# A two-layer hybrid decoder trunk on one core: most tile transposes move from TensorE to VectorE and the DMA queues

## The chip, the cores and the metric

The kernel runs on one core of a Trainium2 chip. The metric is the device time of one execution in microseconds (us). A core has five engines that each take their instructions in order: TensorE (PE; PEld is its weight load), VectorE (DVE), ScalarE (ACT), GpSimd (POOL) and SyncE (SP), which here only issues DMA transfers. The engines wait for each other through semaphores. An instruction that waits holds up everything behind it on its own engine, and a transfer that waits in SP's program holds up every later transfer of SP.

## The reference

Two layers, 256 tokens, model width 2048, everything in float32. Each layer normalises `x`, multiplies it by one wide input projection, and uses the columns for two branches: attention in 16 heads (with query and key normalisation, rotary positions and a mixture of three dilated causal windows), and a causal convolution module (gated unit, depthwise convolution of width 31, layer norm, SiLU, pointwise projection). Both branches are normalised, gated and mapped back into the residual.

```python
for layer in range(DEPTH):
    h = rms_norm(x, norm_g[layer])
    proj = jnp.einsum("bsd,de->bse", h, w_in[layer])
    q, k, v, g_att, glu_a, glu_b, g_conv = jnp.split(proj, SPLIT_POINTS, axis=-1)
    q = apply_rope(rms_norm(q...), cos, sin); k = apply_rope(rms_norm(k...), cos, sin)
    att_y = rms_norm(dilated_mixture(q, k, v), att_out_g[layer]) * jax.nn.silu(g_att)
    conv = conformer_conv(glu_a, glu_b, dw_kernel[layer], ..., w_pw[layer])
    conv_y = rms_norm(conv, conv_out_g[layer]) * jax.nn.silu(g_conv)
    x = x + jnp.einsum("bse,ed->bsd", jnp.concatenate([att_y, conv_y], axis=-1), w_out[layer])
```

## The kernel before, in words

The weights are streamed once. They are cut into 640 tiles of 256 rows by 512 columns (512 KB); eight tiles make a group, which is one block of 512 output columns, and a layer has 40 groups. `load(i)` issues the transfer of tile i on SP into one of four `raw` buffers. `split(i)` turns it into a high part on ACT (`whi`) and a low part on DVE (`wlo`), in one of four pairs of buffers, and then issues `load(i + 4)` into the buffer that it has emptied. TensorE takes 12 matmuls of 512 columns for a tile (high by high, low by high, high by low; two row blocks; two halves of the tokens). The split runs three tiles ahead.

The activations are the stationary operand. They stand transposed, as high and low parts, in `st_hi` and `st_lo` (two sets of four chunks of 512 channels). To make them, and to make `qT`, `kT` and `uT` (the transposed gated unit that the convolution reads), `transposes` sends eight 128 x 128 blocks of a [256, 512] tile through TensorE into two PSUM banks, from which ACT and DVE read. There are 44 such calls: 24 for the gated unit, q and k (4 blocks j in 2 layers each), 8 for g_att, 8 for pw and 4 for the next layer's x.

The order of the groups in a layer is: for j = 0 to 3 the five groups glu_b, glu_a, v, q, k; then g_conv 0, g_att 0 to 3, g_conv 1 to 3, o_att 0 to 3, pw 0 to 3, o_conv 0 to 3. The result of a group is read from PSUM by its `ev_...` function. A group may start only when the group two before it has been read.

Everything that isn't the weight stream is cut into slices that a planner (`Filler`) places. A slice names what it costs on each engine (`Need(A=1.0)`: 1.0 us of ACT), a condition, and the PSUM banks it needs. After every tile the planner's `run` adds each slice that fits its estimate of the engines' clocks, in order of priority. `until` forces slices when the matmuls need their result at once. So the order of each engine's program is fixed when the kernel is built. The convolution (`conv`) has the lowest priority and fills DVE: per block j 124 operations of 128 x 256. When the last block is done, the layer norm follows: a sum over channels on POOL (`ysum`), a matmul with ones, the mean subtracted on DVE, squares on ACT, their sum on POOL (`ssum`, one copy and seven additions), four small matmuls with ones, the reciprocal root on POOL (`rstd`, copied out as `rbc`), two matmuls with `ident` that spread it, then on DVE and ACT the scaling, the SiLU and the parts for `st_hi[1]` and `st_lo[1]`, which the pw groups read. The rotary tables of the next layer are built on POOL with POOL's own transfers (`rope_tables`), and are issued where the code reaches them, at the end of the group o_att 3.

Of the kernel before, what the change touches and what calls it, by code (L numbers as in the profile page):

```python
# [10 lines left out]
F32 = mybir.dt.float32  # L11
F32R = mybir.dt.float32r
BF16 = mybir.dt.bfloat16
AF = mybir.ActivationFunctionType
# [16 lines left out]

KS = 2
NSTEP = KT // KS
R_RAW, R_SPLIT = 4, 4
AHEAD = 3

WARM = 14
# [13 lines left out]
class Filler:  # L51
# [94 lines left out]
def trunk(ctx: ExitStack, tc: tile.TileContext, x, w_in, q_norm_g, k_norm_g, w_pw, w_out, x_t, gains, params,  # L146
# [8 lines left out]
    def t(shape, name, dt=F32):  # L155
        return sb.tile(shape, dt, name=name)
# [13 lines left out]
    qT, kT = (C[i].rearrange("p (h s) -> p h s", h=4) for i in (1, 2))  # L170
    Dt = [t([128, 2, CH], f"d{i}") for i in range(3)]
    t2 = t([128, CH], "t2")
    sm = [t([128, 384], f"sm{i}") for i in range(4)]
    junk = t([128, CH], "junk", BF16)
    ident = t([128, 128], "ident")
# [66 lines left out]
    def has(*what):  # L242
        return lambda: what in flags
# [6 lines left out]
    def transposes(src, banks):  # L250

        for b in range(2):
            for i in range(2):
                for tt in range(2):
                    e = (2 * b + i) * 128
                    T.transpose(banks[b][:, i * SEQ + tt * 128:i * SEQ + tt * 128 + 128],  # L256
                                src[:, tt, e:e + 128], ident)

    def to_stationary(src, s, c, gain):
# [12 lines left out]
        filled(s, c)  # L272

    def filled(s, c):
        vacant[s][c] = False
        ready[s][c] = True
# [11 lines left out]

    def x_chunk(l, c):

        yield from to_stationary(A[c], 0, c, lambda i: ng[:, l * KT + 4 * c + i:l * KT + 4 * c + i + 1])
        fill.add(x_square(l, c), 3, fill.now[4])

    def x_square(l, c):
# [16 lines left out]
    def ev_glu_a(l, j, ps):  # L311
        yield Need(0, has("ev", l, "glu_b", j), V=1.4)
        for tt in range(2):
            V.scalar_tensor_tensor(Dt[0][:, tt], ps[tt], rx[:, tt:tt + 1], Dt[0][:, tt],
                                   op0=ALU.mult, op1=ALU.mult)
        flag("ev", l, "glu_a", j)
        yield Need(2, has("conv", l, j - 2) if j >= 2 else None, P=0.9)
        banks = [fill.bank(), fill.bank()]
        transposes(Dt[0], banks)
        yield Need(A=1.0)  # L320
        for b in range(2):
            S.activation(uT[j % 2][:, 2 * b:2 * b + 2, PAD:], banks[b].rearrange("p (c s) -> p c s", c=2), AF.Copy)
        fill.free(*banks)
        flag("glu", l, j)
        fill.add(conv(l, j), 5 + j, fill.now[4])

# [92 lines left out]
    def ev_qk(l, j, ps, nm):  # L419
        before = ("rope", l, j, "q") if nm == "k" else ("rope", l, j - 1, "k") if j else None  # L420
        yield Need(0, before and has(*before), A=2.8, G=2.3)
        for tt in range(2):
            for h in range(4):
                S.activation(junk[:, :DH], ps[tt][:, h * DH:(h + 1) * DH], AF.Square, scale=rx[:, tt:tt + 1],  # L424
                             accum_out=qss[:, tt, h:h + 1])
        a, b = (1.0, DH * EPS) if nm == "q" else (1.0 / DH, EPS)
        G.tensor_scalar(qr, qss, a, b, op0=ALU.mult, op1=ALU.add)  # L427
        G.tensor_tensor(qr, qr, half.rearrange("p (t h) -> p t h", t=2), op=ALU.pow)  # L428
        G.tensor_mul(qr, qr, rx[:, :, None].to_broadcast([128, 2, 4]))  # L429
        n = Dt[1]  # L430
        for tt in range(2):
            yield Need(A=1.2)
            for h in range(4):
                S.activation(n[:, tt, h * DH:(h + 1) * DH], ps[tt][:, h * DH:(h + 1) * DH], AF.Copy,  # L434
                             scale=qr[:, tt, h:h + 1])
        flag("ev", l, nm, j)
        o = Dt[2]
        for tt in range(2):
            yield Need(V=1.9)
            nt, ot = (z[:, tt].rearrange("p (h d) -> p h d", h=4) for z in (n, o))  # L440
            t2v = t2.rearrange("p (h d) -> p h d", h=4)
            ca, cb = rope[nm + "a"], rope[nm + "b"]
# [6 lines left out]
        banks = [fill.bank(), fill.bank()]  # L449
        transposes(o, banks)  # L450
        flag("rope", l, j, nm)
        yield Need(A=1.0)
        dst = qT if nm == "q" else kT
        for b in range(2):
            S.activation(dst[:, 2 * b:2 * b + 2], banks[b].rearrange("p (h s) -> p h s", h=2), AF.Copy)  # L455
        fill.free(*banks)
        if nm == "k":
            for h in range(4):
                fill.add(head(l, j, h), 2, fill.now[4])

    def head(l, j, h):
        yield Need(1, has("attn", l, j - 1) if j else None, P=0.7)
        ps = fill.bank()
        T.matmul(ps[:, 0:128], qT[:, h, 0:128], kT[:, h, 0:128], start=True, stop=True)  # L464
        T.matmul(ps[:, 128:384], qT[:, h, 128:256], kT[:, h, 0:256], start=True, stop=True)  # L465
        flag("qk1", l, j, h)
        if all(("qk1", l, j, k) in flags for k in range(4)):
            flag("qk", l, j)
# [48 lines left out]
    def ev_g_att(l, j, ps):  # L517
# [5 lines left out]
        yield from to_stationary(A[j], 0, j, lambda i: prm[:, 4 * j + i, P_ATT + l:P_ATT + l + 1])  # L523
# [9 lines left out]
    def ev_pw(l, j, ps):  # L533
# [6 lines left out]
        if j == NCH - 1:  # L540
# [4 lines left out]
        yield from to_stationary(y, 1, j, lambda i: prm[:, 4 * j + i, P_CONV + l:P_CONV + l + 1])  # L545

    def ev_o_conv(l, j, ps):
        yield Need(0, has("rc", l), V=1.4)
# [19 lines left out]
    load(2)  # L568
    nc.sync.dma_start(Y[2], x_t[:, 2])
    load(3)  # L570
    later = [(Y[3], x_t[:, 3], None)]
    later += [(A[c], x[0, :, c * CH:(c + 1) * CH].rearrange("(t p) e -> p t e", p=128), c) for c in range(NCH)]
    later.append((prm, params, None))
    make_identity(nc, ident)
    V.memset(half, -0.5)
# [113 lines left out]
```

## Time and profile before

| | |
|---|---|
| median of 3 runs | 1861.46 us (1860.73 to 1862.61) |
| the profiled execution | 1862.08 us, span 1860.3 us, mean granted TensorE clock 0.998 |
| busy | PE 1847.6 us, DVE 1392.2, ACT 989.2, POOL 140.2 |
| moved by DMA | 352.06 MB, mean 189 GB/s, queue q1 at 60.7% of 16 engines |

The matmuls are pipelined, so a busy PE isn't a PE at its peak; a better view is the chain of work that ended last, which gives the distance from one instruction to the next.

### The profile page before, as it was taken

The page shows a single profiled execution, that of the slowest core. Times are in us where ns is not written, and L with a number is a line of the kernel's source. Part 1 is how long each engine was busy: PE and PEld are TensorE (multiplying, and loading weights), DVE is VectorE, ACT ScalarE, POOL GpSimd, SP SyncE. Part 2 cuts the span into 40 slices and gives each one's busy share as a digit, 9 for nine tenths or more (in the row PEclk, how much of TensorE's full clock was granted, in tenths as well). Part 3 has the DMA queues.
Part 4 walks back from the last instruction along what each step waited for, and adds up shares of the span by engine and source line. Part 5 has one row for each costly group of instructions (what it writes and reads, how often), then busy time and mean ns, then how long its engine had stood idle before and what let it go on. Part 6 is the DMA issues. An engine that isn't in the chain of part 4 may idle for free.

```text
span 1860.3 us, 23725 instructions
## 1 busy us (share of the span) xinstructions
PE 1847.6 (99%) x8490; PEld 1535.9 (83%) x8490; DVE 1392.2 (75%) x2157; ACT 989.2 (53%) x1559; POOL 140.2 (8%) x153
## 2 busy tenths in 40 slices
PE   8999999999999999999999999999999999999999
PEld 6788888888888888888888888888888888888887
DVE  5788889788889876556558888797887998755554
ACT  5565564654654465445444655646556445644542
POOL 2010100200010141000000101002000102100000
PEclk9999999999999999999999999999999999999999
DMA  8765656656566676565666656565565666665564
GB/s 277 218 184 169 183 170 182 182 172 189 170 183 191 193 224 208 195 186 191 210 200 188 191 159 186 162 195 182 161 188 162 196 195 188 213 205 193 180 204 147
DMA packets 181527, 352.06 MB, mean 189 GB/s; under 512 B 11248, under 2 KB 11248, under 8 KB 181408
## 3 DMA queue, kind: packets, MB, share of 16 engines
q1 hardware_dynamic: 179584, 347.19, 60.7%
q0 software_dynamic: 960, 1.77, 0.5%
q8 instruction: 66, 1.08, 0.2%
q10 hardware_dynamic: 864, 1.59, 0.2%
q14 instruction: 53, 0.43, 0.1%
HBM read 346.31 MB, written 4.19 MB: 188 GB/s over the span
## 4 chain that ended last, share of the span: by engine, by line
PE 97%; DMA 1%; DVE 1%; ACT 0%; issue 0%; SPq 0%; POOL 0%; ACTq 0%; DVEq 0%
PE acc L619 92%; PE ax L256 2%; DMA raw<-in_w_in 1%; PE ax L465 1%; DMA a<-in_x 1%; PE ax L482 1%; PE ax L491 0%; PE ax L490 0%; PE ax L489 0%; PE ax L464 0%; DVE wlo L230 0%; ACT whi L229 0%; DVE stlo L285 0%; SPq L222 0%; ACT junk L297 0%
## 5 line engine op out<-in xcount | busy, mean ns | idle before, releaser
L230 DVE TENSOR_TENSOR wlo<-raw,whi 128x1024 fp32r<-128x1024 f32 x640 | 792.6, 1247 | 411.7 <-ACT whi L229 405.6
L229 ACT ACTIVATE whi<-raw 128x1024 fp32r<-128x1024 f32 x640 | 675.4, 1063 | 658.2 <-PE acc L619 468.4
L619 PE MATMUL acc<-whi,sthi 128*128 128x512 f32 x2560 | 823.9, 393 | 6.6 <-ACT sthi L283 5.8
L619 PE MATMUL acc<-wlo,sthi 128*128 128x512 f32 x2560 | 815.9, 390 | 0.8 <-DVE wlo L230 0.8
L619 PE MATMUL acc<-whi,stlo 128*128 128x512 f32 x2560 | 815.5, 390 | 0.0
L619 PEld LDWEIGHTS acc<-wlo,sthi 128*128 128x128 f32 x2560 | 481.2, 188 | 102.3 <-DVE wlo L230 1.8
L619 PEld LDWEIGHTS acc<-whi,stlo 128*128 128x128 f32 x2560 | 481.1, 188 | 100.8
L619 PEld LDWEIGHTS acc<-whi,sthi 128*128 128x128 f32 x2560 | 476.5, 188 | 102.8 <-ACT sthi L283 6.7
L339 DVE SCALAR_TENSOR_TENSOR y<-ut,prm,y 128x256 f32<-128x256 f32 x960 | 408.4, 482 | 0.0
L427 POOL TENSOR_SCALAR qr<-qss 128x8 f32<-128x8 f32 x16 | 3.2, 198 | 696.6 <-ACT junk L424 696.6
L347 POOL TENSOR_TENSOR ysum<-ysum,y 128x256 f32<-128x256 f32 x30 | 36.5, 1218 | 240.8 <-DVE y L339 133.5
L424 ACT ACTIVATE junk<-acc,rx 128x128 bf16<-128x128 f32 x128 | 47.1, 368 | 8.4 <-PE acc L619 4.8
L434 ACT ACTIVATE d<-acc,qr 128x128 f32<-128x128 f32 x128 | 34.8, 384 | 15.8 <-POOL qr L429 15.8
L267 ACT ACTIVATE sthi<-ax,prm 128x256 fp32r<-128x256 f32 x64 | 25.1, 476 | 30.7 <-PE ax L256 30.7
L269 DVE SCALAR_TENSOR_TENSOR stlo<-ax,prm,sthi 128x256 fp32r<-128x256 f32 x64 | 26.5, 475 | 14.4 <-ACT sthi L267 14.4
L455 ACT ACTIVATE c<-ax 128x512 f32<-128x512 f32 x32 | 17.4, 597 | 33.7 <-PE ax L256 33.7
L478 ACT ACTIVATE sm<-sm,smm 128x128 f32<-128x128 f32 x64 | 28.2, 443 | 6.6 <-DVE smm L473 6.6
L375 POOL TENSOR_TENSOR ssum<-ssum,d 128x512 f32<-128x512 f32 x14 | 28.5, 2034 | 6.5 <-ACT d L368 5.6
L428 POOL TENSOR_TENSOR qr<-qr,half 128x8 f32<-128x8 f32 x16 | 26.3, 1642 | 1.3
L256 PEld LDWEIGHTS ax<-ident,d 128*128 128x128 f32 x192 | 22.4, 140 | 3.2
L256 PE MATMUL ax<-ident,d 128*128 128x128 f32 x192 | 24.9, 273 | 0.0
L424 ACT ACTIVATION_READ_ACCUMULATOR junk<-acc,rx 128x1 f32 x128 | 24.7, 193 | 0.0
(105 smaller groups left out, 659.2 us busy)
## 6 DMA issues: line engine op xcount, KB each, us to landing
raw<-in_w_in SPq DMA_DIRECT2D x448, 512.0 KB, 4.1
raw<-in_w_out SPq DMA_DIRECT2D x128, 512.0 KB, 4.7
raw<-in_w_pw SPq DMA_DIRECT2D x64, 512.0 KB, 4.7
a<-in_x SPq DMA_DIRECT2D x8, 512.0 KB, 6.1
xs<-a SPq DMA_DIRECT2D x4, 512.0 KB, 7.0
a<-xs SPq DMA_DIRECT2D x4, 512.0 KB, 6.1
y<-in_x_t SPq DMA_DIRECT2D x3, 512.0 KB, 12.5
out<-a SPq DMA_DIRECT2D x4, 256.0 KB, 5.4
```

The lines of the kernel that those rows point to most:

```text
L229: S.activation(hi, a, AF.Copy)
L230: V.tensor_sub(wlo[i % R_SPLIT], a, hi.bitcast(F32))
L256: T.transpose(banks[b][:, i * SEQ + tt * 128:i * SEQ + tt * 128 + 128], src[:, tt, e:e + 128], ident)
L269: V.scalar_tensor_tensor(st_lo[s][c][:, i], p[i], gain(i), st_hi[s][c][:, i].bitcast(F32), op0=ALU.mult, op1=ALU.subtract)
L339: V.scalar_tensor_tensor(y[:, c], u[:, c, k:k + SEQ], w[:, c, l * CW + k:l * CW + k + 1], y[:, c], op0=ALU.mult, op1=ALU.add)
L347: G.tensor_add(ysum, ysum, y[:, c])
L375: G.tensor_add(ssum, ssum, half_sq)
L424: S.activation(junk[:, :DH], ps[tt][:, h * DH:(h + 1) * DH], AF.Square, scale=rx[:, tt:tt + 1], accum_out=qss[:, tt, h:h + 1])
L428: G.tensor_tensor(qr, qr, half.rearrange("p (t h) -> p t h", t=2), op=ALU.pow)
L434: S.activation(n[:, tt, h * DH:(h + 1) * DH], ps[tt][:, h * DH:(h + 1) * DH], AF.Copy, scale=qr[:, tt, h:h + 1])
L478: S.activation(s[:, cs], s[:, cs], AF.Exp, bias=m[:, tt:tt + 1], scale=-1.0, accum_out=lsum[:, tt:tt + 1])
L619: T.matmul(ps[tt], xl if n == 2 else xh, lo[:, kk] if n == 1 else hi[:, kk], start=(k == 0 and n == 0), stop=(k == KT - 1 and n == 2))
```

## The change

Of the 44 calls of `transposes`, 41 are replaced by `turn`; the three that stay are the last x chunk and pw 3 of both layers. (The words of the change count 296 of 320 blocks; in the code it is 328 of 352.) `turn` transposes the 32 x 32 squares inside a [256, 512] tile on DVE (two instructions, into the one buffer `blocks`), stores the result to DRAM with one transfer of 512 KB in rows of 1 KB, and brings it back with four loads of 128 KB, each of which puts one 32-row block of the squares at its place on all partitions. All five transfers are issued on SP. `turned` is the view in which the result is then read: its tokens lie in runs of 32. ACT and DVE read SBUF where they read PSUM; `kT` needs no copy, since the head matmuls read the loaded tile itself. A flag lets only one turn be between its transposes and its loads in the planner's order. The planner has a new clock, Q, for the exchange. Six `raw` buffers take the place of four, six tiles are loaded at the start, and the last chunk of `x_t` is loaded before them rather than among the later loads. The buffer for POOL's transfer descriptors is set to 4096.

```diff
-R_RAW, R_SPLIT = 4, 4
+R_RAW, R_SPLIT = 6, 4
...
-        self.t = dict(P=0.0, V=0.0, A=0.0, G=0.0)
+        self.t = dict(P=0.0, V=0.0, A=0.0, G=0.0, Q=0.0)
...
+    def turn(src, dst):
+        yield Need(0, lambda: not turns[1], V=1.4)
+        turns[1] = True
+        for tt in range(2):
+            V.transpose(blocks.rearrange("p (b c t j) -> p t c b j", b=4, c=4, t=2)[:, tt],
+                        src[:, tt].rearrange("p (c b j) -> p c b j", c=4, b=4))
+        yield Need(Q=6.0)
+        way = crossing[turns[0] % 2]
+        turns[0] += 1
+        nc.sync.dma_start(way.rearrange("b p x -> p b x"), blocks.rearrange("p (b x) -> p b x", b=4))
+        yield Need(Q=7.0)
+        turns[1] = False
+        for a in range(4):
+            nc.sync.dma_start(dst[:, a * SEQ:(a + 1) * SEQ], way[:, 32 * a:32 * a + 32])
+
+    def turned(z):
+        return z.rearrange("p (a c t j) -> p c t a j", a=4, c=4, t=2)
+
+    def to_stationary_turned(src, dst, s, c, gain):
+        yield from turn(src, dst)
+        yield Need(0, lambda: vacant[s][c], A=1.8, V=2.2)
+        z = turned(dst)
...
+        for i in range(4):
+            S.activation(hi[:, i], z[:, i], AF.Copy, scale=gain(i))
+        for i in range(4):
+            for tt in range(2):
+                V.scalar_tensor_tensor(lo[:, i, tt], z[:, i, tt], gain(i), hi[:, i, tt].bitcast(F32),
...
-        yield Need(2, has("qk", l, j - 1) if j else None, P=0.9)
-        banks = [fill.bank(), fill.bank()]
-        transposes(o, banks)
+        before = has("qk", l, j - 1) if j else None
+        if nm == "q":
+            z = o.rearrange("p t e -> p (t e)")
+            yield from turn(o, z)
+            yield Need(0, before, A=1.8)
+            for h in range(4):
+                S.activation(qT[:, h].rearrange("p (t a j) -> p t a j", t=2, a=4), turned(z)[:, h], AF.Copy)
+        else:
+            yield Need(0, before)
+            yield from turn(o, kT)
...
-    later = [(Y[3], x_t[:, 3], None)]
+    load(4)
+    nc.sync.dma_start(Y[3], x_t[:, 3])
+    load(5)
...
+    nc = bacc.Bacc("TRN2", target_bir_lowering=False, num_devices=1, dynamic_dma_scratch_size=4096)
```

Three places show how the planner's order comes out. The tiles are numbered through from 0; pw 0 of the first layer begins with tile 256.

First place: POOL's program in the first layer, from the sum of the layer norm (`ysum`, `ssum`) to `rbc`. Before:

```order
L347 TENSOR_TENSOR ysum<-ysum,y_84 128x256 x4
L373 COPY ssum<-d_108 128x512
L375 TENSOR_TENSOR ssum<-ssum,d_108 128x512
L375 TENSOR_TENSOR ssum<-ssum,d_109 128x512 x2
L375 TENSOR_TENSOR ssum<-ssum,d_108 128x512 x2
L375 TENSOR_TENSOR ssum<-ssum,d_109 128x512 x2
L247 TENSOR_SCALAR rstd<-rsc 128x2
L248 TENSOR_TENSOR rstd<-rstd,half 128x2
L389 COPY rbc<-rstd 128x256
L583 DMA ropeqa<-in_rope_cos 128x2x128
L586 DMA gbc<-in_q_norm_g 128x64 x2
L588 TENSOR_TENSOR ropeqa<-ropeqa,gbc 128x256
```

Now (of the rotary tables only the first and the last of the four are shown):

```order
L389 TENSOR_TENSOR ysum<-ysum,y_84 128x256 x4
L415 COPY ssum<-d_110 128x512
L417 TENSOR_TENSOR ssum<-ssum,d_110 128x512
L417 TENSOR_TENSOR ssum<-ssum,d_111 128x512 x2
L636 DMA ropeqa<-in_rope_cos 128x2x128
L639 DMA gbc<-in_q_norm_g 128x64 x2
...
L641 TENSOR_TENSOR ropekb<-ropekb,gbc 128x256
L417 TENSOR_TENSOR ssum<-ssum,d_110 128x512 x2
L417 TENSOR_TENSOR ssum<-ssum,d_111 128x512 x2
L251 TENSOR_SCALAR rstd<-rsc 128x2
L252 TENSOR_TENSOR rstd<-rstd,half 128x2
L431 COPY rbc<-rstd 128x256
```

Before, the sum and the root were whole ahead of the tables; now all four tables stand between its fourth and its fifth operation. In the second layer there are no tables to build, and the eight operations stand together.

Second place: PE's program at the layer norm's small matmuls (`ones,ssum` and `ident,rbc`). Before, in the group o_att 0 of the first layer, ahead of tile 227 (the second pair, not shown, stood ahead of tile 231):

```order
L619 MATMUL acc_153<-whi_95,stlo_74 128x512
L619 MATMUL acc_154<-whi_95,stlo_74 128x512
L383 MATMUL ax_158<-ones,ssum 128x2 x4
L619 MATMUL acc_153<-whi_96,sthi_66 128x512
L619 MATMUL acc_154<-whi_96,sthi_66 128x512
```

Now:

```order
L672 MATMUL acc_159<-wlo_102,sthi_68 128x512
L672 MATMUL acc_159<-whi_98,stlo_76 128x512
L425 MATMUL ax_161<-ones,ssum 128x2 x4
L435 MATMUL ax_162<-ident,rbc 128x128 x2
L672 MATMUL acc_156<-whi_95,sthi_69 128x512
L672 MATMUL acc_157<-whi_95,sthi_69 128x512
L672 MATMUL acc_156<-wlo_99,sthi_69 128x512
```

Both pairs now stand directly ahead of tile 256, whose first matmul reads `sthi_69`, the layer norm's own result; in the second layer they stand the same way ahead of tile 576. The matmul that sums `ysum` stood ahead of tile 216 (536) and stands ahead of tile 250 (570). On DVE the last operation of the convolution stood behind 215 splits of a layer's 320 and stands behind 249.

Third place: SP's program round the turn of k for j = 0 (`crossing` is the DRAM buffer, `c_107` is `kT`; the last load shown ahead of the store is that of tile 59):

```order
L226 DMA raw_93<-in_w_in 128x2x512
L226 DMA raw_94<-in_w_in 128x2x512
L275 DMA crossing_164<-blocks 128x4x256
L279 DMA c_107<-crossing_164 128x1x256 x4
L226 DMA raw_89<-in_w_in 128x2x512
L226 DMA raw_90<-in_w_in 128x2x512
```

Before, only weight loads stood here. The head matmuls that read `kT` stood one tile behind k's transposes on PE (the tile between them was 46); now they stand ahead of tile 56, and wait for the four loads. The pattern repeats every 40 tiles, eight times in all.

## Rows read from the trace of the kernel before

**Rows 1.** The page: busy us (share of the span) xinstructions, and DVE's largest group.
```profile
PE 1847.6 (99%) x8490; PEld 1535.9 (83%) x8490; DVE 1392.2 (75%) x2157; ACT 989.2 (53%) x1559; POOL 140.2 (8%) x153
L230 DVE TENSOR_TENSOR wlo<-raw,whi 128x1024 fp32r<-128x1024 f32 x640 | 792.6, 1247 | 411.7 <-ACT whi L229 405.6
```
**Rows 2.** The chain that ended last, by line: share of the span.
```profile
PE acc L619 92%; PE ax L256 2%; DMA raw<-in_w_in 1%; PE ax L465 1%; DMA a<-in_x 1%; PE ax L482 1%; PE ax L491 0%; PE ax L490 0%; PE ax L489 0%; PE ax L464 0%; DVE wlo L230 0%; ACT whi L229 0%; DVE stlo L285 0%; SPq L222 0%; ACT junk L297 0%
```
**Rows 3.** The chain in order of time, 640 to 720 us: start us, us, what.
```profile
643.73 0.43 PE ax L355 x2
649.65 0.87 PE ax L256 x8
650.52 5.49 PE acc L619 x24
...
677.72 0.79 PE ax L383 x8
...
689.51 0.45 PE ax L393 x4
```
**Rows 4.** Groups by form: busy us, mean ns of one, idle before (TensorE's transposes).
```profile
L256 PE MATMUL ax<-ident,d 128*128 128x128 f32 x192 | 24.9, 273 | 0.0
L256 PE MATMUL ax<-ident,a 128*128 128x128 f32 x96 | 12.4, 272 | 0.0
L256 PE MATMUL ax<-ident,y 128*128 128x128 f32 x64 | 8.3, 272 | 0.0
```
**Rows 5.** POOL's timeline, 630 to 800 us: start us, us, line, what, idle before.
```profile
652.71 0.61 POOL L373 COPY ssum<-d 128x512 f32<-128x512 f32 x1 [16.12 <-ACT d L368]
653.40 10.23 POOL L375 TENSOR_TENSOR ssum<-ssum,d 128x512 f32<-128x512 f32 x5
...
680.24 0.19 POOL L247 TENSOR_SCALAR rstd<-rsc 128x2 f32<-128x2 f32 x1 [9.42 <-DVE rsc L386]
...
681.62 0.81 POOL L583 DMA_DIRECT2D ropeqa<-in_rope_cos  x1
...
708.92 1.28 POOL L588 TENSOR_TENSOR ropekb<-ropekb,gbc 128x256 f32<-128x256 f32 x1 [3.16 <-DMA gbc<-in_k_norm_g]
```
**Rows 6.** Groups by form on DVE and ACT, whole span.
```profile
L443 DVE TENSOR_TENSOR d<-d,ropeqa 128x512 f32<-128x512 f32 x16 | 10.9, 681 | 0.0
L445 DVE TENSOR_TENSOR t<-d,ropekb 128x256 f32<-128x256 f32 x32 | 12.0, 417 | 0.0
L365 DVE TENSOR_TENSOR y<-y,nmean 128x1024 f32<-128x1024 f32 x8 | 9.8, 1271 | 0.0
L406 ACT ACTIVATE y<-y,prm 128x256 f32<-128x256 f32 x32 | 16.6, 590 | 1.3 <-DVE y L403 1.3
L409 ACT ACTIVATE sthi<-y 128x1024 fp32r<-128x1024 f32 x8 | 8.4, 1053 | 0.1
```
**Rows 7.** The page's DMA issues: xcount, KB each, median us to landing.
```profile
raw<-in_w_in SPq DMA_DIRECT2D x448, 512.0 KB, 4.1
xs<-a SPq DMA_DIRECT2D x4, 512.0 KB, 7.0
ropeka<-in_rope_cos POOLq DMA_DIRECT2D x2, 128.0 KB, 3.5
```
**Rows 8.** ACT's timeline, 244 to 256 us (k is read from PSUM).
```profile
245.97 0.37 ACT L424 ACTIVATE junk<-acc,rx 128x128 bf16<-128x128 f32 x1 [0.30 <-PE acc L619]
...
253.30 2.18 ACT L434 ACTIVATE d<-acc,qr 128x128 f32<-128x128 f32 x8 [1.54 <-POOL qr L429]
```
**Rows 9.** PE's first wait in the timeline, and busy time by window with clock, DMA share, GB/s.
```profile
19.70 1.22 PE L619 MATMUL acc<-whi,sthi 128*128 128x512 f32 x2 [3.66 <-ACT sthi L283]
20.00:30.00 10.00, 10.00 (x39) 8.13 (x39) 9.33 (x16) 7.00 (x14) 4.76 (x7) 0.87 0.94 311
```
**Rows 10.** ACT's timeline, 0 to 60 us: the second chunk of x.
```profile
36.86 0.63 ACT L297 ACTIVATE junk<-a 128x512 bf16<-128x512 f32 x1 [3.08 <-DMA a<-in_x]
```

More of the change, by code (lines that the diff above doesn't have):

```diff
@@ L169, in trunk @@
     VT = [GC[0], GC[3]]
-    qT, kT = (C[i].rearrange("p (h s) -> p h s", h=4) for i in (1, 2))
+    qT, kT = C[1].rearrange("p (h s) -> p h s", h=4), C[2]
     Dt = [t([128, 2, CH], f"d{i}") for i in range(3)]
     t2 = t([128, CH], "t2")
+    blocks = t([128, 2 * CH], "blocks")
     sm = [t([128, 384], f"sm{i}") for i in range(4)]
@@ L197, in trunk @@
     fill = Filler([pp.tile([128, CH], F32, name=f"ax{i}") for i in range(4)], dict(V=4.5, A=3.5), 5)
+    crossing = [dr.tile([4, 128, SEQ], F32, name=f"crossing{i}") for i in range(2)]
+    turns = [0, False]
     xs = [dr.tile([SEQ, CH], F32, name=f"xs{c}") for c in range(NCH)]
@@ L257, in transposes @@
                                 src[:, tt, e:e + 128], ident)
+    def turn(src, dst):
[18 more added lines that the diff above has]
+        z = turned(dst)
+        hi, lo = (o[s][c].rearrange("p c (t a j) -> p c t a j", t=2, a=4) for o in (st_hi, st_lo))
+        for i in range(4):
[3 more added lines that the diff above has]
+                V.scalar_tensor_tensor(lo[:, i, tt], z[:, i, tt], gain(i), hi[:, i, tt].bitcast(F32),
+                                       op0=ALU.mult, op1=ALU.subtract)
+        filled(s, c)
     def to_stationary(src, s, c, gain):
@@ L289, in x_chunk @@
     def x_chunk(l, c):
-        yield from to_stationary(A[c], 0, c, lambda i: ng[:, l * KT + 4 * c + i:l * KT + 4 * c + i + 1])
+        gain = lambda i: ng[:, l * KT + 4 * c + i:l * KT + 4 * c + i + 1]
+        if c < NCH - 1:
+            yield from to_stationary_turned(A[c], Y[c], 0, c, gain)
+        else:
+            yield from to_stationary(A[c], 0, c, gain)
         fill.add(x_square(l, c), 3, fill.now[4])
@@ L316, in ev_glu_a @@
         flag("ev", l, "glu_a", j)
-        yield Need(2, has("conv", l, j - 2) if j >= 2 else None, P=0.9)
-        banks = [fill.bank(), fill.bank()]
[L319 to L323, printed above, removed]
+        z = Dt[0].rearrange("p t e -> p (t e)")
+        yield from turn(Dt[0], z)
+        yield Need(0, has("conv", l, j - 2) if j >= 2 else None, A=1.7)
+        for c in range(4):
+            S.activation(uT[j % 2][:, c, PAD:].rearrange("p (t a j) -> p t a j", t=2, a=4), turned(z)[:, c], AF.Copy)
         flag("glu", l, j)
@@ L447, in ev_qk @@
             V.tensor_add(ot, ot, t2v)
-        yield Need(2, has("qk", l, j - 1) if j else None, P=0.9)
-        banks = [fill.bank(), fill.bank()]
-        transposes(o, banks)
-        flag("rope", l, j, nm)
[L452 to L456, printed above, removed]
+        before = has("qk", l, j - 1) if j else None
[5 more added lines that the diff above has]
+                S.activation(qT[:, h].rearrange("p (t a j) -> p t a j", t=2, a=4), turned(z)[:, h], AF.Copy)
+        else:
+            yield Need(0, before)
+            yield from turn(o, kT)
+        flag("rope", l, j, nm)
+        yield Need()
         if nm == "k":
@@ L463, in head @@
         ps = fill.bank()
-        T.matmul(ps[:, 0:128], qT[:, h, 0:128], kT[:, h, 0:128], start=True, stop=True)
-        T.matmul(ps[:, 128:384], qT[:, h, 128:256], kT[:, h, 0:256], start=True, stop=True)
+        k = turned(kT)[:, h]
+        T.matmul(ps[:, 0:128], qT[:, h, 0:128], k[:, 0], start=True, stop=True)
+        T.matmul(ps[:, 128:384], qT[:, h, 128:256], k, start=True, stop=True)
         flag("qk1", l, j, h)
@@ L522, in ev_g_att @@
         flag("ev", l, "g_att", j)
-        yield from to_stationary(A[j], 0, j, lambda i: prm[:, 4 * j + i, P_ATT + l:P_ATT + l + 1])
+        yield from to_stationary_turned(A[j], A[j].rearrange("p t e -> p (t e)"), 0, j,
+                                        lambda i: prm[:, 4 * j + i, P_ATT + l:P_ATT + l + 1])
         src = x[0, :, j * CH:(j + 1) * CH] if l == 0 else xs[j]
@@ L544, in ev_pw @@
             flag("rc", l)
-        yield from to_stationary(y, 1, j, lambda i: prm[:, 4 * j + i, P_CONV + l:P_CONV + l + 1])
+        gain = lambda i: prm[:, 4 * j + i, P_CONV + l:P_CONV + l + 1]
+        if j < NCH - 1:
+            yield from to_stationary_turned(y, Y[j], 1, j, gain)
+        else:
+            yield from to_stationary(y, 1, j, gain)
     def ev_o_conv(l, j, ps):
@@ L570, in trunk @@
     load(3)
-    later = [(Y[3], x_t[:, 3], None)]
-    later += [(A[c], x[0, :, c * CH:(c + 1) * CH].rearrange("(t p) e -> p t e", p=128), c) for c in range(NCH)]
+    load(4)
+    nc.sync.dma_start(Y[3], x_t[:, 3])
+    load(5)
+    later = [(A[c], x[0, :, c * CH:(c + 1) * CH].rearrange("(t p) e -> p t e", p=128), c) for c in range(NCH)]
     later.append((prm, params, None))
```

1 line of the change is left out of this document (removed).

## The prediction

> **What bounds the kernel now.** I read the page's busy times first. TensorE is busy 99% of the span and no other engine over 75% [rows 1]. The chain that ended last, by line, puts 92% of the span on the weight matmuls and 2% on the transposes of L256 [rows 2]. So the bound is TensorE's program itself, and an instruction taken out of it is worth its place in the chain. In order of time the chain shows that place: eight transposes take 0.87 us, and 24 matmuls (two tiles) 5.49, so a tile is 2.73 us [rows 3]. I then read what could make TensorE wait afterwards: the prices on POOL, DVE and ACT [rows 5, 6], the transfers [rows 7], and the first 60 us, the only part where it waits now [rows 9, 10]. Last I laid the order of the changed program beside these prices.
>
> **What goes.** The transposes are 192 + 96 + 64 = 352 [rows 4], 44 calls of eight; 41 calls go: 41 x 0.87 = **35.7 us less** on the path. No other engine takes these 35.7 us onto the path by its busy time: DVE gains 82 square transposes and some small operations.
>
> **Price of a square transpose.** No row shows one. A 128 x 512 operation of two operands takes 0.68 us, half that length 0.42, twice that length 1.27 [rows 6]. I take 0.68, the row of the same size, and keep 0.42 and 1.27 as ends. 82 x 0.68 = 56 us. The low parts in eight pieces of 128 in place of four of 256 add little. DVE goes from 1392 to about 1455 us, still under 80%.
>
> [...] No run here shows a square transpose.
>
> **The layer norm comes to the start of pw.** This decides my forecast. More work for DVE at higher priority pushes the convolution back: its last operation moves from behind split 215 to behind split 249, and with it all that follows. In the new order the matmul that sums `ysum` is ahead of tile 250, and both pairs of small matmuls stand directly ahead of tile 256, which reads the norm's result. TensorE works in order, so it stands from the end of tile 255 until the norm is through. I count from the start of tile 250; without the norm tile 256 starts 6 x 2.73 = 16.4 us later.
> - Mean on ACT 0.6; one split on ACT and DVE 2.1; the first subtraction 1.27 [rows 6]; the first square 1.1, which is as long as L409 [rows 6]: 5.1 us.
> - POOL: a copy 0.61, and each addition 10.23 / 5 = 2.05 [rows 5]. The first four of the eight operations end at 5.1 + 0.6 + 6.2 = 12 us.
> - In the first layer the four rotary tables are next. They took from 681.62 to 708.92 + 1.28, 28.6 us, most of it waiting for POOL's own transfers [rows 5]. Then four additions, 8.2: the sum ends at 48.8 us. In the second layer it ends at 20.2 us.
> - Then one after the other: small matmuls 0.8 [rows 3]; copy and root 1.6 (680.24 to 681.62 [rows 5] and the copy); spread 0.5 [rows 3]; mean row 0.5; scaling 1.3; the SiLU of two chunks, 8 x 0.52 = 4.2 (0.59 each, overlapping [rows 6]); the high part 1.1 [rows 6]: 10.0 us with the hops.
>
> Tile 256 starts at 58.8 us in place of 16.4. Of this 1.2 us is work that was there before: **41 us**. Tile 576: 30.2 - 16.4 - 1.2 = **12.6 us**. ACT has the SiLU of two more chunks and two splits, one of which needs tile 256 done, ahead of the second chunk's high part. So tile 258 waits again, 3.7 us by the same prices. [...] Sum of both layers: 41 + 12.6 + 2 x 3.7 + 4 x 1.5 = **67 us more**. Bounds: if the transfers of the tables meet empty queues and the additions run at 1.4 us beside an idle DVE, 45; if the tables take 34 us and the waits cost more clock, 78. The smaller descriptor buffer of POOL's transfers lay beside idle time before and would now add to the tables; I cost it at nothing within that bound.
>
> **The exchange and the head matmuls.** k's heads now wait for a store, four issues and four loads. The store is the nearest to xs<-a, 512 KB, 7.0 us; a load of 128 KB took 3.5, of 512 KB 4.1 [rows 7]; four issues 1.5. I take 12.0 us from the store's issue to the last landing, with 9 and 15 as ends (the rows of 128 KB and of 7.0 with and without queueing). The room: ACT takes up q's copies when tile 43 starts, and the heads stand 13 tiles later, 35.4 us. In between stand a split and the copies 3.0, reading k 9.5 (245.97 to 255.48 [rows 8]), then on DVE five splits 1.15 apart (1.247 busy [rows 1]) and the wait for the first's high part 1.1, two halves of rotary 2.0 each [rows 6], two square transposes 1.3, and on SP the load of tile 59 ahead of the store 0.5: 25.1 us. 25.1 + 12.0 - 35.4 = 1.7 us, eight times: **14 us more** (0 to 45). q's own copies have 12.7 us for the exchange, so at 12.0 they cost nothing; the gated unit's blocks ACT longer, but the inserted head matmuls give it the time.
>
> [...]
>
> **The weight stream.** During an exchange SP issues nothing else for about 9 us, three tiles. With six buffers the next load is 6.7 us late and lands about 3 us before its split would start. I cost it at nothing; with only four buffers it would be late. The new traffic, 41 x 1 MB on 352, finds a queue at 60.7% of the DMA engines. The head matmuls read `kT` in runs of 32 now; I cost that at nothing, and if it doubled the matmuls of L465 it would be 1% of the span [rows 2].
>
> **The start.** ACT now has both first chunks of x ahead of split 7; before, the second stood behind split 8 and landed at 36.8 [rows 10]. As many bytes stand ahead of it as before, and the queues are full (0.94 [rows 9]), so it lands at about 35.5. Two squarings and split 7 end near 38.6; tile 7 is due at 34.8. With what follows, less the 1.6 us wait that is there now: **5 us more** (-2 to 9).
>
> **Sum.** The profiled execution took 1862.1 us, 0.6 above the median of three. 1862.1 - 35.7 + 67 + 14 + 5 = 1912.4; on the median's footing **1912 us**.
>
> **The rivals.**
> - *The exchange is covered.* If it takes 10 us or less, the heads wait for nothing; with a start that costs nothing, 1862 - 36 + 67 = 1893. For it: the new loads are small and meet short queues. Against it: the 7.0 us row. With the norm's lower bound as well, 1871. [...]
> - *The exchange is slow.* At 15 us q's copies come 2.3 us too late, the heads wait 5.6 us and ACT another 2: 10 x 8 = 80 in place of 14, 1978. For it: rows of 1 KB, and SP's queue; against it: no landing in the steady part of the trace is so long.
> - *Not slower: POOL is much quicker than its rows when DVE stands.* The place is POOL between the first square and `rbc`. Its price by the rows is 45 us in the first layer and 16 in the second, 61 together. The path loses 35.7 us, so with the heads covered and the start at nothing this work would have to shrink to about 30 us; at 20 us the time is 1852. For it: the tables' transfers wait beside a full weight stream now, and would not then. Against it: 61 us halved.
>
> **How the numbers follow.** The forecast's case (1898 to 1930) has 0.55, the covered exchange (1870 to 1898) 0.22, the slow one (1930 to 1980) 0.18, the last rival 0.05. For 8 in 10 I take the first, most of the second and the near part of the third: 1884 to 1940. 0.2% (3.7 us) is what a measurement can tell from no change. Faster: 0.03 of the last rival; same: 0.02; slower: all else, 0.95.
>
> **What would show it.** Right: in the chain of waits TensorE waits some 40 us ahead of the first pw group and 13 ahead of the second, for POOL's `ssum`, `rbc` and then ACT's `sthi`; POOL's tables lie inside the first; the granted clock falls there; the head matmuls wait for a DMA eight times, by 1 to 3 us; tile distances elsewhere stay at 2.73. Wrong: no such wait at pw; heads that wait over 4 us; ACT waiting for `raw` in the steady part; a square transpose far from 0.68 us.

## The result and the profile after

The changed kernel takes 2015.0 us (median of 4 runs, 2013.5 to 2018.4) against 1861.1 for the kernel before: 1.083 times as long, 95% interval 1.081 to 1.084. The direction was forecast; the size was not. The time lies 103 us above the forecast of 1912 and outside its range.

I read the page of the changed kernel first: busy time, and granted clock by slices.

```profile
span 2012.6 us, 23527 instructions
PE 1862.5 (93%) x8162; PEld 1528.4 (76%) x8162; DVE 1441.1 (72%) x2307; ACT 990.0 (49%) x1575; POOL 137.7 (7%) x153
PEclk9999999989999999599989999999899999997999
```

TensorE has 328 instructions fewer, all of them gone as planned, and yet it is busy 15 us longer than before (1847.6 in [rows 1]). It stands still for 2012.6 - 1862.5 = 150 us, against 13 before. So the loss has two parts: waits, and the same work done more slowly. The slices of 9 in the clock fall to 5 at slice 16 (counted from 0; 805 to 855 us), to 7 at slice 36, and to 8 at slices 8, 20 and 28. I then asked what TensorE waited for (us in total, times, longest; the longest entries of the view):

```profile
PE ax L510 <- DMA c<-crossing: 51.3, 8, 8.4
PE ax L425 <- POOL ssum L417: 31.3, 2, 26.4
PE acc L672 <- ACT sthi L451: 20.0, 4, 6.8
PE acc L672 <- ACT whi L233: 14.5, 12, 2.1
PE acc L672 <- DVE wlo L234: 8.4, 12, 0.8
PE ax L260 <- DVE a L601: 6.2, 2, 6.1
PE acc L672 <- ACT sthi L323: 6.1, 2, 4.8
PE ax L435 <- POOL rbc L431: 3.6, 2, 1.8
```

L510 is the first head matmul, L425 and L435 are the norm's small matmuls, L672 the weight matmuls. The second, third and last rows are the layer norm ahead of pw, as forecast: 55 us in two layers. The first is the exchange: eight head groups wait 6.4 us each, where 1.7 had been forecast. The fourth to sixth had no place in the forecast at all. They are splits and a last x chunk that come late. The seventh is the start, about as long as before (5.8 us). ACT's own waits say why the splits are late:

```profile
ACT c L496 <- DMA d<-crossing: 38.2, 8, 5.5
ACT ut L365 <- DMA d<-crossing: 36.5, 6, 7.6
ACT sthi L292 <- DMA y<-crossing: 33.6, 5, 9.2
...
ACT whi L233 <- DMA raw<-in_w_in: 21.6, 16, 4.5
```

ACT stands in its own order for exchanged blocks (q's copies, the gated unit, x and pw), and the next split stands behind it.

The chain of work that ended last, at the first of the eight k exchanges (start us, us, what; pieces under 0.1 us are left out), shows where such a wait, here 6.8 us, comes from:

```profile
165.83 1.30 DVE blocks L270 x2
167.13 2.24 DVE wlo L234 x2
...
169.81 6.14 DMA crossing<-blocks
175.97 0.54 SPq L279
...
177.67 8.40 DMA c<-crossing
186.21 0.77 PE ax L510 x2
```

From the store's issue (169.81) to the last landing (177.67 + 8.40 = 186.07) are 16.3 us; 12.0 had been forecast. The store took 6.1 where 7.0 stood in [rows 7], the issues were about as estimated, and the last load took 8.4 us where the row of equal size had 3.5. The store also stands 2.7 us behind the squares on DVE, because SP has a weight load ahead of it that waits for a split.

The norm ahead of pw in the first layer came in the order that was worked out, with POOL's tables (L636 to L641) inside its sum:

```profile
787.60 1.58 POOL ssum L415
...
791.51 2.17 POOL ssum L417
...
795.89 0.74 POOL ropeqa L636
...
819.45 0.72 POOL ropekb L641
820.17 1.22 POOL ssum L417
...
825.46 1.89 PE ax L425 x8
...
847.62 0.95 ACT sthi L451
```

Last, the slow clock. Behind a head wait of 6.8 us (it ends at 186.21) the window reads: width, busy us of PE, PEld, DVE, ACT, POOL, clock, DMA share, GB/s.

```profile
186.20:192.00 5.80, 5.79 (x20) 5.08 (x21) 2.58 (x17) 3.21 (x14) 0.00 (x0) 0.60 0.58 215
192.00:200.00 8.00, 8.00 (x43) 6.75 (x42) 4.12 (x7) 4.31 (x10) 0.00 (x0) 1.00 0.44 133
```

With a granted clock of 0.60 over 5.8 us, I estimate 0.40 x 5.8 = 2.3 us of work lost, on top of the wait. The head matmuls lie just there, and by form (busy us, mean ns of one) they take 49.7 us, where they took 31.4 before:

```profile
L511 PE MATMUL ax<-c,c 128*128 128x256 f32 x64 | 29.4, 556 | 0.0
L510 PE MATMUL ax<-c,c 128*128 128x128 f32 x64 | 20.3, 417 | 51.3 <-DMA c<-crossing 51.3
```

### The profile page after: what moved, and what is told of

Read it like the earlier page. It is cut to its first block, busy times and chain, and to the rows that moved or that the text cites. A ratio compares the mean times of both kernels' runs of the same rounds, so it can differ in the third digit from the quotient of the medians.

```text
span 2012.6 us, 23527 instructions
## 1 busy us (share of the span) xinstructions
PE 1862.5 (93%) x8162; PEld 1528.4 (76%) x8162; DVE 1441.1 (72%) x2307; ACT 990.0 (49%) x1575; POOL 137.7 (7%) x153
## 4 chain that ended last, share of the span: by engine, by line
PE 58%; DMA 18%; DVE 9%; ACT 6%; issue 4%; POOL 3%; SPq 2%; ACTq 0%; DVEq 0%; POOLq 0%
PE acc L672 54%; DMA crossing<-blocks 6%; DVE wlo L234 4%; DMA c<-crossing 3%; DMA d<-crossing 3%; ACT junk L466 2%; SPq L279 2%; DMA y<-crossing 2%; DVE y L381 1%; ACT whi L233 1%; PE ax L511 1%; DMA raw<-in_w_in 1%; POOL ssum L417 1%; DMA raw<-in_w_pw 1%; DVE t L487 1%
## 5 line engine op out<-in xcount | busy, mean ns | idle before, releaser
L672 PE MATMUL acc<-whi,sthi 128*128 128x512 f32 x2560 | 830.7, 396 | 41.8 <-ACT sthi L451 20.0
L672 PE MATMUL acc<-wlo,sthi 128*128 128x512 f32 x2560 | 824.4, 393 | 8.5 <-DVE wlo L234 8.4
L672 PE MATMUL acc<-whi,stlo 128*128 128x512 f32 x2560 | 822.2, 392 | 0.0
L672 PEld LDWEIGHTS acc<-whi,sthi 128*128 128x128 f32 x2560 | 484.3, 190 | 150.1 <-ACT sthi L451 21.4
L672 PEld LDWEIGHTS acc<-wlo,sthi 128*128 128x128 f32 x2560 | 485.2, 190 | 116.2 <-DVE wlo L234 14.6
L672 PEld LDWEIGHTS acc<-whi,stlo 128*128 128x128 f32 x2560 | 484.9, 190 | 103.1 <-DVE stlo L452 1.5
L510 PE MATMUL ax<-c,c 128*128 128x128 f32 x64 | 20.3, 417 | 51.3 <-DMA c<-crossing 51.3
L510 PEld LDWEIGHTS ax<-c,c 128*128 128x128 f32 x64 | 19.0, 312 | 58.4 <-issue 45.7
L519 DVE CUSTOM_DVE_ANT_0 sm<-ax,mask 128x128 f32<-128x128 f32 x64 | 20.4, 356 | 46.9 <-PE ax L511 46.8
L476 ACT ACTIVATE d<-acc,qr 128x128 f32<-128x128 f32 x128 | 34.7, 383 | 19.1 <-POOL qr L471 19.1
L425 PE MATMUL ax<-ones,ssum 128*128 128x2 f32 x16 | 3.4, 331 | 31.3 <-POOL ssum L417 31.3
L365 ACT ACTIVATE ut<-d 128x256 f32<-128x256 f32 x32 | 11.3, 409 | 41.7 <-DMA d<-crossing 36.5
L270 DVE STREAM_TRANSPOSE blocks<-d 128x512 f32<-128x512 f32 x48 | 31.1, 688 | 0.0
L496 ACT ACTIVATE c<-d 128x256 f32<-128x256 f32 x32 | 10.7, 405 | 38.2 <-DMA d<-crossing 38.2
L511 PE MATMUL ax<-c,c 128*128 128x256 f32 x64 | 29.4, 556 | 0.0
```

Source lines behind the costliest of these rows:

```text
L270: V.transpose(blocks.rearrange("p (b c t j) -> p t c b j", b=4, c=4, t=2)[:, tt], src[:, tt].rearrange("p (c b j) -> p c b j", c=4, b=4))
L510: T.matmul(ps[:, 0:128], qT[:, h, 0:128], k[:, 0], start=True, stop=True)
L511: T.matmul(ps[:, 128:384], qT[:, h, 128:256], k, start=True, stop=True)
L672: T.matmul(ps[tt], xl if n == 2 else xh, lo[:, kk] if n == 1 else hi[:, kk], start=(k == 0 and n == 0), stop=(k == KT - 1 and n == 2))
```

## The experiments

All edits are of the changed kernel, except where the text names the kernel before. "Not busy" is the span less TensorE's busy time, both from the page of each run. From E1 to E7, E10 and E11 TensorE has the same 8162 instructions as in the changed kernel, so a difference in its busy time is its speed. E6, E8 and E10 are medians of 4 runs and E9 of 7; E1 to E5, E7 and E11 were run once, and there a few us (the four runs of the changed kernel lie 5 us apart) can't be told from nothing.

| | time us | PE busy | not busy |
|---|---|---|---|
| before | 1861.1 | 1847.6 | 12.7 |
| after | 2015.0 | 1862.5 | 150.1 |
| E1 loads by 32 rows | 1898.0 | 1825.1 | 71.1 |
| E2 tables later | 1998.1 | 1867.1 | 129.2 |
| E3 convolution's rank | 2130.9 | 1869.3 | 259.8 |
| E4 = E1 + E3 | 2056.4 | 1860.0 | 194.7 |
| E5 tile priced 2.73 | 1953.1 | 1853.5 | 97.8 |
| E6 = E1 + E5 | 1835.7 | 1816.0 | 18.1 |
| E7 loads of 2 rows | 2222.9 | 1917.5 | 303.6 |
| E8 before, tile priced 2.73 | 1869.8 | 1851.0 | 16.4 |
| E9 before, start alone | 1867.4 | 1849.6 | 16.0 |
| E10 = E6 + exchange priced 9 | 1832.4 | 1813.8 | 18.0 |
| E11 = E5 + exchange priced 13 | 1885.9 | 1834.0 | 50.2 |

**E1: the same bytes, loads cut the other way.**

```diff
-        for a in range(4):
-            nc.sync.dma_start(dst[:, a * SEQ:(a + 1) * SEQ], way[:, 32 * a:32 * a + 32])
+        for b in range(4):
+            nc.sync.dma_start(dst[32 * b:32 * b + 32].rearrange("j (a x) -> j a x", a=4),
+                              way[b].rearrange("(a j) x -> j a x", a=4))
```

> The four loads of an exchange carry the same bytes in the same rows of 1 KB, but are cut by blocks of 32 output partitions, so that the outermost dimension of each is 32 rows and not 4; the order on every engine is the changed kernel's. Theory A (a load whose outermost dimension is 4 is worked off by about 4 of the 16 DMA engines: during the loads of the exchange at 138.5 us about 94 packets of 46 ns started per us, 4.3 engines' worth, against 232 to 297 per us in the store): the last load lands in about 3.5 us in place of 8.1, the head matmuls wait under 1 us each in place of 6.4, ACT's waits for exchanged blocks and the splits that come late behind them go too. Of the 152 us of span that the change cost, 51 are the heads' waits, about 16 the slow clock after them, about 24 the late splits and about 10 the two places where the next layer's last chunk waits: time 1905 to 1935 us. Theory B (the loads are late because they read what was just stored, or because they stand among the weight loads in one queue): landing stays at 7 to 8 us and the time at 2000 to 2020 us.

1898.0 us: theory A, and 7 us better than its range. The page's DMA issues give a median of 2.5 or 2.6 us to landing for each kind of these loads, here k's:

```profile
c<-crossing SPq DMA_DIRECT2D x32, 128.0 KB, 2.6
```

No head waits any more, and what TensorE still waits for is above all the norm, unchanged:

```profile
PE ax L426 <- POOL ssum L418: 31.2, 2, 26.3
PE acc L673 <- ACT sthi L452: 20.1, 4, 6.8
...
PE ax L436 <- POOL rbc L432: 3.6, 2, 1.8
```

The 117 us are 79 of standing (150.1 - 71.1) and 37 of slower work (1862.5 - 1825.1). Added up over the stretches in which TensorE is busy, what the granted clock lacks of 1 makes 43.1 us in the changed kernel and 12.9 here, so 30 of the 37 are the clock. The late splits (14.5 and 8.4 us fall to 2.5 and 2.3) and the wait at L260 (6.2 us, now none) go with the heads' waits: they were ACT and DVE standing in their own order behind exchanged blocks. The head matmuls are back at the times of the kernel before (19.1 and 12.3 us), though they still read `kT` in runs of 32, so those runs cost nothing:

```profile
L512 PE MATMUL ax<-c,c 128*128 128x256 f32 x64 | 19.1, 380 | 0.0
L511 PE MATMUL ax<-c,c 128*128 128x128 f32 x64 | 12.4, 276 | 0.1
```

**E7: the dose.** If the outermost dimension decides, two rows must be worse than four.

```diff
-            nc.sync.dma_start(dst[:, a * SEQ:(a + 1) * SEQ], way[:, 32 * a:32 * a + 32])
+            for b in (0, 2):
+                nc.sync.dma_start(dst[32 * b:32 * b + 64, a * SEQ:(a + 1) * SEQ], way[b:b + 2, 32 * a:32 * a + 32])
```

> The changed kernel with each load of an exchange split in two, of 2 rows by 32 each: eight loads of 64 KB with an outermost dimension of 2, the same bytes in the same rows of 1 KB. Theory A (the outermost dimension sets how many DMA engines work on a load): about 45 packets start per us in place of 94, the 512 packets take about 11.8 us, the last load lands some 13 us after the first issue, the head matmuls wait 9 to 11 us each in place of 6.4: 2040 to 2090 us. Rival B (how many partitions a load writes, or how much of it lies together in DRAM, decides; smaller loads land sooner): only four issues of 0.57 us more, 2005 to 2035 us.

2222.9 us: theory A in the mechanism, though the time is 133 us above its range. The heads wait 10.4 to 11.5 us, where 9 to 11 had been expected. Left out were the late splits, 111 us where the changed kernel had 14.5, and TensorE's speed: it is busy 55 us longer than in the changed kernel:

```profile
PE acc L673 <- ACT whi L233: 110.7, 27, 9.1
PE ax L511 <- DMA c<-crossing: 54.8, 5, 11.4
PE ax L511 <- DMA raw<-in_w_in: 34.0, 3, 11.5
```

The dose is plainest in windows in which almost nothing but the loads of q's first exchange moves (the last two numbers are the DMA share and GB/s). With an outermost dimension of 2, of 4 (the changed kernel) and of 32 (E1):

```profile
145.00:151.00 6.00, 6.00 (x28) 4.99 (x27) 3.94 (x6) 1.40 (x2) 0.00 (x0) 1.00 0.13 47
```
```profile
138.80:140.30 1.50, 1.50 (x8) 1.27 (x7) 0.80 (x2) 0.77 (x1) 0.00 (x0) 1.00 0.23 76
```
```profile
137.20:138.80 1.60, 1.60 (x9) 1.33 (x8) 0.89 (x3) 1.06 (x1) 0.00 (x0) 1.00 0.88 259
```

Shares of 0.13, 0.23 and 0.88 of 16 engines are as much as 2, 4 and 14 engines at work. A share is a mean, so I also give how many packets of 1 KB the traces have under way at once: 2.1 (to 149.5 us), 4.3 (from 139.5 on) and 13.8. A packet takes 46 ns (median) in all three, so only the number under way differs. In the changed kernel several loads are on their way there, and the 4.3 packets are those of all of them together. The two runs also take apart what E1 changed together: its loads write 32 partitions each and read one block of DRAM, but E7's write 64 in place of 128 and are slower (47 GB/s for 76). So fewer partitions or smaller loads are not what helped.

**E2: the rotary tables out of the norm's way.**

```diff
-            if nm == "o_att" and j == NCH - 1 and l + 1 < DEPTH:
+            if nm == "pw" and j == 1 and l + 1 < DEPTH:
                 rope_tables(l + 1)
```

> The second layer's rotary tables are issued on POOL after the second pw group in place of after the last o_att group, so they no longer stand inside POOL's sum of squares. Theory A (the sum of squares sets the start of pw, and the tables' 24.3 us on POOL, 795.9 to 820.2, lie on that path): TensorE's wait for ssum in the first layer falls from 26.4 us to the second layer's 4.9, time 1990 to 1996 us. Rival B (ACT's squarings or the additions beside DVE would end nearly as late): the wait stays above 20 us and the time at 2008 to 2018 us.

1998.1 us, 2 us above A's range. The wait itself does what A says: from 26.4 to 4.9 us.

```profile
PE ax L425 <- POOL ssum L417: 9.8, 2, 4.9
```

But the time falls by 17 and not by 21: 2 us come back at L260, which now waits 8.4 where it waited 6.1, and TensorE is busy 5 us longer. So the tables were worth 21 us of waiting. That the time fell by less rests on one run and is within the 5 us by which runs of the changed kernel differ.

**E3 and E4: the convolution's rank.**

```diff
-        fill.add(conv(l, j), 5 + j, fill.now[4])
+        fill.add(conv(l, j), 3, fill.now[4])
```

> Only the planner's rank of the convolution is raised (3 for every chunk in place of 5 to 8). The matmul of the norm's mean then stands ahead of tile 233 and the small matmuls of its deviation ahead of tiles 248 and 250, pw's first tile being 256; and the head matmuls come six tiles (16.4 us) later than in the changed kernel. The exchange is as slow as there. Theory A (the cost lies in where the norm and the heads stand, and an exchange of 16 us is harmless with 16 us more room): no wait ahead of pw (55 us of waiting and 12 of slow clock less) and none at the heads (51 and 16 less), the late splits stay: 1870 to 1900 us. Rival B (DVE has no room: what the convolution takes, the rotary halves and square blocks lose, and the heads or the gates wait as long as before): 1940 to 2000 us.

> Loads cut by 32 rows and the convolution's rank raised, together. Theory A (two separate causes that add): the late splits go too, and what is left is the kernel before less 31 to 36 us of transposes and plus a few us of start and waits: 1835 to 1865 us. Rival B (one shared cause, DVE's or the queue's load, moves elsewhere): above 1880 us.

2130.9 and 2056.4 us: theory A is refuted in both, and rival B is right in kind but 131 us too low for E3. The norm's waits are gone, and the heads' with the slow loads are down to 7.1 us. A new wait takes their place, first E3, then E4:

```profile
PE acc L672 <- ACT d L476: 199.1, 28, 23.1
```
```profile
PE acc L673 <- ACT d L477: 164.6, 28, 18.9
```

L476 (L477 in E4) is the reading of q and k from PSUM. A convolution ahead of the rotary halves pushes q's exchange back to where k's bank is needed again, and then everything stands in one line, here in E4 (pieces under 0.1 us are left out):

```profile
291.71 1.31 DVE blocks L270 x2
293.04 3.88 DMA crossing<-blocks
...
298.26 2.70 DMA d<-crossing
...
301.07 1.34 ACT c L497 x4
...
308.59 2.19 ACT d L477 x8
...
310.82 3.33 PE acc L673 x7
```

With fast loads TensorE waits less for it (164.6 us in place of 199.1), but the line isn't covered. So it isn't enough that the norm comes early; what is pushed aside for it counts.

**E5 and E6: the planner's price of a tile.** The planner counted 2.6 us for a tile that takes 2.73 ([rows 3] has 5.49 for two). Before, each call of `transposes` also put 0.9 us on its clock of TensorE, where it took 0.87, and that price left with the calls. What its leaving alone did to the norm's place was not tried; the edit puts the same clock right by the price of a tile.

```diff
-        fill.use([("P", 2.6)], halved[i])
+        fill.use([("P", 2.73)], halved[i])
```

> The changed kernel with one number of the planner altered: it counts a tile of matmuls at 2.73 us, as the trace shows it, in place of 2.6. The matmul of the norm's mean then stands ahead of tile 220 and its deviation's ahead of tiles 234 and 236; the loads of the exchange stay in four rows. Theory A (norm and exchange are two separate costs): the 55 us of waiting at the two pw stages and about 12 us of slow clock go, the heads' waits of 51 us stay: 1940 to 1960 us. Rival B (DVE's time is short, so a convolution that ends sooner costs the heads or the readers of q and k as much, as when its rank was raised): 1990 us or more.

> Loads cut by 32 rows, and the planner counts 2.73 us for a tile. Theory A (the two costs add and nothing else of size is left): from 1898 us with the loads alone, 55 us of waiting at pw and about 11 us of slow clock less: 1832 us, 1825 to 1842, so 20 to 36 us under the kernel before. Rival B (a third cost takes their place at the heads or at the gates): above 1855 us.

1953.1 and 1835.7 us: theory A in both. The norm's waits vanish from E5, the heads' stay (49.6 us, 8 times):

```profile
PE ax L510 <- DMA c<-crossing: 49.6, 8, 7.3
```

The norm at the start of pw is thus worth 2015.0 - 1953.1 = 62 us, and 1898.0 - 1835.7 = 62 beside fast loads. The edit moves other slices too, but the trace puts the gain where the norm stood: 55 us of waits for it are gone, TensorE stands 52 us less in all (150.1 - 97.8) and is busy 9 us less (1862.5 - 1853.5). The two costs add: 117 + 62 = 179 us, and 2015.0 - 1835.7 is 179. E6 beats the kernel before: 0.986, interval 0.984 to 0.988.

**E8: that price in the kernel before.**

> The kernel before, with the planner counting 2.73 us for a tile. The norm's mean moves from ahead of tile 216 to ahead of tile 197. Theory A (TensorE waits for nothing there, so an earlier norm is worth nothing): within 3 us of the kernel before. Rival B (the planner's number is worth something by itself, and a gain of the combined version over the kernel before would be its doing): over 5 us faster.

1869.8 us, ratio 1.004 (1.0025 to 1.0055). Neither theory foresaw a loss. B is out: E6 doesn't owe its gain to the number alone. Most of the 7 us (1862.7 for the kernel before beside it) arises early: in the first 80 us TensorE has 268 instructions where the kernel before has 291. Which slice does it was not tried.

**E9: the start alone, in the kernel before.** Six `raw` buffers, the changed order of the first transfers, the smaller descriptor buffer.

> The kernel before with three small parts of the change alone: six weight tiles on their way in place of four, the transfers of the start in the changed order, and the smaller descriptor buffer for POOL's transfers. Theory A (the trace after shows 11.1 us of waits in the first 56 us against 8.0 before, and 2 us less under the slow clock): 0 to 4 us slower than the kernel before. Rival B (the prediction's term: split 7 late behind both first chunks): 5 us slower or more. Rival C (six buffers help the steady part): faster by over 2 us.

1867.4 us against 1861.7 for the kernel before beside it, ratio 1.0029 (1.0018 to 1.0041): 5.7 us slower, in rival B's range, though the interval (3.4 to 7.6 us) doesn't quite shut out theory A. The three parts were not taken apart. TensorE stands 3.3 us longer (16.0 against 12.7) and is busy 2.0 us longer, so a reading of its waits alone misses a part. Of the waits, 0.8 us at 36.48 stand behind the second chunk of x, as forecast; 1.5 and 0.5 us at 40.82 and 42.08 stand behind the third chunk, which ACT now also squares ahead of a split (38.35).

**E10: an exchange priced at 9 us.** E6 with one more number:

```diff
-        yield Need(Q=7.0)
+        yield Need(Q=9)
```

> Loads by 32 rows, 2.73 us for a tile, and the planner counts 9 us in place of 7 from the issue of an exchange's store to its landing, which sets the heads ahead of tiles 57, 97, 137, 177 in place of 56, 95, 135, 175. Theory A (the 4.4 us that the heads still wait in the combined version go, with a little slow clock): 1826 to 1834 us. Rival B (what is left is the start and TensorE's own work): within 3 us of 1836.

1832.4 us, ratio 0.984 (0.983 to 0.986): in theory A's range, and in the trace the heads wait for nothing. By the time alone it isn't told from E6, whose interval overlaps. It has the lowest median, 29 us under the kernel before.

**E11: slow loads, honestly priced.** E5 with `Q=13.0`.

> The changed kernel with its loads in four rows, but with a planner that counts 2.73 us for a tile and 13 us in place of 7 from an exchange's store to its landing: the heads stand ahead of tiles 59, 100, 140, 180, three to five tiles later than in the changed kernel. Theory A (a slow exchange costs nothing where the order leaves it its 16 us): the heads' waits go, the late splits behind ACT's waits for the exchange stay: 1860 to 1890 us. Rival B (loads on four DMA engines hurt even so, through the weight stream and ACT's place in the order): above 1900 us.

1885.9 us, within A's range, but what is left is rival B's. The heads' waits and ACT's for the exchange are gone. ACT waits for weight loads now, and TensorE for ACT's reading of k behind them:

```profile
ACT whi L233 <- DMA raw<-in_w_in: 82.3, 32, 6.3
...
PE acc L672 <- ACT d L476: 35.6, 16, 5.8
```

One such weight load shows in the chain as landing over 9 us (259.76 to 268.94), where [rows 7] had a median of 4.1. In E10, with the loads cut by 32 rows, ACT waits for weights 2 times and 3.0 us. So the planner's price is worth 1953.1 - 1885.9 = 67 us with the slow loads, and the slow loads still cost the weight stream. E11 is 53 us behind E10, which differs in the price too (9 for 13). The packets of the trace show the crowding itself: from 262 to 266 us, 4.4 packets of 1 KB (the exchange's) are under way at once and 12.5 of 2 KB (the weights'); once the exchange is through, from 267 to 269, it is 16.8 of 2 KB. So until then the weight loads have a quarter fewer packets under way.

## Why the prediction was wrong, point by point

- **The transposes that leave**: right. E10, which waits about as little as the kernel before, has TensorE busy for 1813.8 us against 1847.6: 33.8 less, 35.7 forecast.
- **A square transpose at 0.68 us**: right, 688 ns. Taking the row of the same size was a guess that came true; no row of the kernel before showed one.

```profile
L270 DVE STREAM_TRANSPOSE blocks<-d 128x512 f32<-128x512 f32 x48 | 31.1, 688 | 0.0
```

- **The layer norm, 67 us**: right in place and size, 62 by E5 and by E6. Two parts missed in opposite ways: 61 us of waits had been forecast and 55 came, 6 of slow work and 9 came. No run shows that term of 6, 1.5 us behind each of four waits; what the runs show is TensorE busy 9 us less in E5, where these waits are gone, and in the changed kernel a granted clock of 0.55 from 837.10 to 843.40, right behind one of them, by my estimate 0.45 x 6.3 = 2.8 us lost. The tables took 24.3 us on POOL (795.89 to 820.17) for the 28.6 of the rows, and the additions behind them 1.2 to 1.3 us beside an idle DVE. The second wait of each layer and the slow clock were there: in the first layer a pair of matmuls takes 1.22 us right after the first wait and 0.61 at 843.49, and the second wait, 3.15 us, follows at 848.62.

```profile
837.10 1.22 PE L672 MATMUL acc<-whi,sthi 128*128 128x512 f32 x2 [6.75 <-ACT sthi L451]
...
843.49 0.61 PE L672 MATMUL acc<-whi,stlo 128*128 128x512 f32 x2
```

- **The start, 5 us**: right in size, 5.7 by E9, and in part by luck. The working gave 38.6 - 34.8 - 1.6 = 2.2 us and left the other 2.8 to "what follows". In E9 the second chunk is taken up at 32.74, not at 35.5, and the longest of the new waits stands behind the third chunk, which the working didn't name.
- **The exchange and the head matmuls, 14 us**: this step failed, in "a load of 128 KB took 3.5, of 512 KB 4.1 ... I take 12.0 us". It measured 117 us (after less E1). The working around it held where nothing else is late: in E1 the store's issue comes 24.3 us after tile 43 starts and the heads' place 35.5 us after it, for 25.1 and 35.4 in the forecast. In the changed kernel the same two distances are 28.8 and 38.4 us at the first exchange, because ACT waits 4.4 us for q's exchange, which the forecast had covered, and splits come late. Being 3.7 and 3.0 us longer they nearly cancel, so that 25.1 + 16.3 - 35.4 = 6.0 us still comes near the measured 6.4. What failed is the row that was chosen by bytes. The loads of [rows 7] have 128 rows outermost; those of the exchange have 4, and all four loads together had a share of 0.23 where almost nothing else moved, and 4.3 packets under way: as much as 4 of the 16 DMA engines at work. E1 and E7 show it from both sides (0.88 with 32 rows, 0.13 with 2). In E1 the exchange takes 164.31 to about 174.5, 10.2 us, and costs nothing: that is the rival of the covered exchange, forecast at 1893, measured at 1898.
- **The slow exchange as a rival, 1978**: the right case with too low a price. It held the heads' waits and 2 us for ACT. It lacked the splits and the last x chunk that stand behind a waiting ACT and DVE, and the clock: 37 of the 117 us are TensorE doing the same work more slowly, where 1.5 us were given to each of four waits and none to the heads'. Its own sum is loose as well: 25.1 + 15 - 35.4 is 4.7 us and not 5.6, and 5.6 + 2 makes 10 only with the 2.3 us of q's copies added.
- **The weight stream at nothing**: wrong with loads of four rows. ACT waits for weights 16 times in the changed kernel, 21.6 us, mostly hidden behind its other waits, and 82.3 us in E11, where those are gone. **`kT` in runs of 32 at nothing**: right, by E1.

With 117 in place of 14, the forecast's sum is 1912 + 103 = 2015. The miss is that one term, with small errors beside it that nearly cancel: the measured terms give 1861.1 - 33.8 + 62 + 117 + 5.7 = 2012.

## What to carry to other kernels

Price a transfer by its shape before its size: look at the outermost dimension (here 2, 4 and 32 rows gave 47, 76 and 259 GB/s), and in the trace at the DMA share while it runs alone. When work leaves an engine, look at what a planner charged for it, since its clock for everything else shifts with it. And here a wait of TensorE cost more than its length (6.8 us, then a granted clock of 0.60 for 5.8 us): read the granted clock behind it, and look for what stands in order behind the engines that wait.

## What was not expected of the hardware

- The same 8162 instructions keep TensorE busy for 1813.8 us in E10 and 1862.5 in the changed kernel. Of these 49 us the granted clock makes 40: what it lacks of 1 while TensorE is busy adds up to 3.3 us in E10 and 43.1 in the changed kernel. Where the other 9 arise is open.
- Eight loads of 64 KB with two rows outermost run at 47 GB/s, four of 128 KB with 32 rows at 259; four rows give 76.
- An addition of 128 x 512 on POOL took 2.17 us at 791.51, while DVE made splits (790.19 to 799.25), and 1.22 at 820.17, while DVE had nothing to do (800.57 to 827.37). No run varied this alone.
